# A gated decoder block on one core: x, parameters and weights laid out in the order in which the kernel reads them

## The chip, the cores and the metric

The kernel runs on one core of one Trainium2 chip. The metric is the device time of one execution in microseconds. The profiler records one execution: when each instruction of each engine ran, what ended its waits, and what the core's 16 DMA engines moved. The engines are called as in the profile: PE (TensorE, matmuls), PEld (its weight loads), DVE (VectorE), ACT (ScalarE), POOL (GpSimd) and SP (SyncE, which here only issues DMAs).

## The reference

One decoder block on x of 1 x 256 x 4096 in float32, cut to what matters (b, s, d are batch, sequence and channels; `w_in` is 4096 x 20480, `w_branch` 2 x 2048 x 4096, `w_out` 4096 x 4096):

```python
h = rmsnorm(x, norm_w)                     # over the 4096 channels of a token
proj = h @ w_in
u_p, z_p, u_c, b_c, c_c, z_c, g_logit = split(proj, ...)   # six of 2048, one of 8192
y_pool = causal_multiscale_pool(u_p, pool_w, pool_scale) * silu(z_p)
y_conv = causal_gated_shortconv(u_c, b_c, c_c, conv_w, conv_b) * silu(z_c)
br = einsum('bsnc,ncd->bsnd', stack([y_pool, y_conv], axis=2), w_branch)
gates = sigmoid(g_logit.reshape(b, s, 2, d) + gate_b)
x = x + sum(gates * br, axis=2) @ w_out
return rmsnorm(x, final_norm_w)
```

## The kernel before

Every large product is cut into units of 1024 output columns: 20 units of `w_in`, 8 of `w_branch`, 4 of `w_out`, run one after the other. A unit is a list of steps (class `Step`). A step takes 256 rows of the weights by 1024 columns, which is one megabyte, and multiplies them with the matching 256 channels of the operand for all 256 tokens.

Float32 accuracy comes from splitting each number into a high part (rounded to `F32R` by ACT) and a low part (the rest, by a DVE subtraction), and from three products: high by high, high by low, low by high. A matmul is 128 x 128 by 512 columns. A step of kind **P** does 24 of them. A step of kind **S** does the same 256 x 1024 block with seven products in place of eight (Strassen-like sums of blocks of the operand and of the weights), 21 matmuls, and needs sums of blocks on both sides: `Q3`, `Q5`, `Q6`, `Q7` of the operand, made once for each operand by `sums_s`, and sums of weights, made by DVE for each step. A step of kind **N**, in the first unit only, is a P step whose two halves of k go to different banks (24 matmuls).

The operand x lies in `arena` as `x_ops`: 16 pairs of blocks of 128 channels, 9 in P form, 7 in a form that S steps can use. P form is x times `norm_w`, not yet divided by the root mean square of the token; that factor, `rin`, is applied when the sums are taken out of PSUM (`evacuate`). For the S form the sums that go to the shared banks must hold the factor already (`rbc` and `std`: the factor and its inverse, spread over partitions by PE at L968).

The order of the work is written out when the program is built. `pump` prepares steps up to three ahead of the one that PE runs (`AHEAD`): it issues the load of the step's megabyte on SP's queue into one of three `raw` buffers (`issue_load`; the buffer must have been prepared three steps before), and lets ACT and DVE write the high and low parts into `ring`, a ring of 60 blocks of 256 columns, of which a P step needs 16. Work that is to lie ahead of a step's preparation is hung on it with `before(i, fn)`. Lines L65 (`act`), L68 (`tt`), L80 (`stt`), L83 (`load`) and L87 (`move`, POOL's queue) are helpers, so most operations carry one of these lines, and L1158 is the one line of all matmuls of steps.

In the first unit x itself is still to be turned. x is loaded by tokens (256 rows of 4096), into the homes `R`, `E`, `Y` and again `R`, a quarter each; for each pair p, `turn(p)` (L980) has PE transpose four 128 x 128 blocks into PSUM, and `x_direct` (pairs 0 to 9) writes high and low parts from there. Pairs 10 to 15 are turned by `x_stage`, stored back, and made into S form by `x_sums` and `x_fill`, the N steps of the first unit using them. Pair 9 is made into S form by `x_second` at step 19. `square` makes the sums of squares of the tokens from x by tokens, on ACT and DVE. `norm_w`, `conv_w` and `conv_b` are loaded as rows of 128 and transposed by PE (L933, L937). `make_bands` builds the masks for the pooling on POOL and DVE, at step 21. From the second unit on (`cc0`, whose six S steps are steps 21, 23 and so on to 31) the matmuls are all P and S steps.

Of the kernel before, what the change touches and what calls it, by code (L numbers as in the profile page):

```python
# [56 lines left out]
def hybrid_block(ctx: ExitStack, tc: tile.TileContext, x, norm_w, w_in, pool_w, pool_scale,  # L57
                 conv_w, conv_b, gate_b, w_branch, w_out, final_norm_w, out):
    nc = tc.nc
    xf, of = x[0], out[0]  # L60
    win, wbr, wout, pw = w_in[0], w_branch[0], w_out[0], pool_w[0]
# [51 lines left out]
    ssq = sb("ssq", [P, 2, 8])  # L113
# [20 lines left out]
    def xs(a, b, t=None):  # L134
        q = xhome[a // NU]
        s = slice(a % NU, (b - 1) % NU + 1)
        return q[:, :, s] if t is None else q[:, t, s]

    def load_x(a, b, queue=None):
        pin((queue or nc.sync).dma_start(xs(a, b), xrows[:, :, a:b]))  # L140
# [15 lines left out]
    rows, ones, std = (op.tile([P, P], F32, name=n) for n in ("rows", "ones", "std"))  # L156
    rbc = op.tile([P, T], F32, name="rbc")
    warm = V[:, 0, 0:P].bitcast(BF16)
    rows_n = V[0:32, 1, 0:P]
# [65 lines left out]
    class Step:  # L225
        def __init__(self, unit, kind, src=None, op=None, **kw):
            self.unit, self.kind, self.src, self.op = unit, kind, src, op
            self.__dict__.update(kw)
            self.raw = None
            self.ending = False  # L230
            self.pre = []

        def micros(self):
# [3 lines left out]
            def half(n):  # L237
                def f(block):
# [14 lines left out]
            if self.kind in "PN":  # L253
                self.blocks, self.h, self.l = [None] * 2, [None] * 2, [None] * 2
                return self.pre + [(8, None, half(0)), (8, None, half(1))]
            if self.kind == "S":
# [29 lines left out]
                return self.pre + [(0, None, sums), (12, None, direct), (8, None, t13), (8, None, t24)]  # L286
# [31 lines left out]
        def groups(self):  # L318

            gs = []  # L320
            if self in steps[0:2]:

                for n in range(2):
                    for i in range(3):
                        for k in range(2):
# [5 lines left out]
            elif self.kind in "PN":  # L331
# [3 lines left out]
                for t, n in order:  # L335
                    mm = {"E": [], "F": []}
                    for k in range(2):
                        ah, al = self.op.standing(k, t)
                        h, l = self.h[n][:, k], self.l[n][:, k]
                        mm["F" if self.kind == "N" and k == 0 else "E"] += [(ah, h), (ah, l), (al, h)]  # L340
                    gs += [[(b, t, n), mm[b], None] for b in "FE" if mm[b]]
# [24 lines left out]
    class Unit:  # L366
        def __init__(self, name, src, seq, ops, epi, scaled=False, before=None, dst=None):
# [5 lines left out]
            for kind, i in seq:  # L373
                if kind in "PSN":
                    self.steps.append(Step(self, kind, src(i).rearrange("(k p) n -> p k n", p=P), ops[i],
# [3 lines left out]
                elif kind == "M":  # L379
                    self.steps.append(Step(self, "M", pw[i].rearrange("(k p) n -> p k n", p=P), g=i % 2))  # L380
            self.s = any(st.kind == "S" for st in self.steps)
            self.n = any(st.kind == "N" for st in self.steps)
            main = [st for st in self.steps if st.kind in "PSN"]
# [3 lines left out]
            for st in main:  # L387
                if st.kind in "PN":
                    for t in range(2):
                        for n in range(2):  # L390
                            for k in "FE":
                                b = (k, t, n)
                                more = (6 if k == "E" else 0) if st.kind == "P" else 3
                                self.total[b] = self.total.get(b, 0) + more
# [18 lines left out]
    def evacuate(u, t):  # L413

        dst = E if u.s or u.n else u.dst
# [27 lines left out]
    def combine(u):  # L443
# [9 lines left out]
        elif u.n:  # L453
            for i in range(4):
                cs = slice((i % 2) * NH, (i % 2 + 1) * NH)
                add(d[:, i // 2, cs], shared(i), E[:, i // 2, cs])
# [70 lines left out]
    for o in all_ops:  # L527
        o.standing = standing_p(o)
    for i in range(NP_X, NP_X + NB):
        x_ops[i].standing = standing_s(x_ops[i], ((7, 8), (A12, A22)))  # L530
# [36 lines left out]
    seq_0 = [("P", i) for i in range(NP_X + NB)] + [("N", i) for i in range(NP_X + NB, NP_X + NS_X)]  # L567
# [821 lines left out]
```

## Time and profile before

| | |
|---|---|
| median of 3 runs | 2405.05 us (2404.59 to 2405.11) |
| the profiled execution | 2405.06 us, span 2403.4 us |
| busy PE, DVE, ACT, POOL (share of the span) | 99%, 87%, 56%, 3% |
| DMA | 538.73 MB, mean 224 GB/s |
| granted TensorE clock, mean | 0.999 |

The span goes from the first to the last instruction. A group's line gives engine, operation, out<-in and the count (x), then busy time, the mean ns of one, and the idle time of the engine just before with its releaser. PE's ends are modelled and overlap, so a matmul's mean is longer than the distance between two. The windows view lists, for a stretch, the busy time and the count of each engine, then the granted clock, the DMA engines' busy share and GB/s. The timeline gives start, length, engine, line, operation, tiles and count; in brackets stands the idle time before it and who ended it.

### The profile page before, as it was taken

What the parts mean: (1) busy time and instruction counts of PE and PEld (TensorE: products, weight loads), DVE (VectorE), ACT (ScalarE), POOL (GpSimd) and SP (SyncE); (2) the same over time, 40 slices, a digit from 0 to 9 for tenths busy, and PEclk for the clock granted to TensorE, in tenths of its full rate; (3) what the DMA queues carried; (4) which work ended last, traced back from release to release, by engine and by line L of the source; (5) the groups of instructions that cost most, each with busy time, mean ns of one, the idle gap of its engine ahead of it and who ended that gap; (6) DMA issues with size and microseconds to landing.
All of it is one profiled execution on the core that took longest, in us unless ns stands there. A gap on an engine that the chain in (4) does not pass through costs nothing.

```text
span 2403.4 us, 27936 instructions
## 1 busy us (share of the span) xinstructions
PE 2388.5 (99%) x10666; PEld 1976.7 (82%) x10666; DVE 2095.2 (87%) x2090; ACT 1353.5 (56%) x1406; POOL 62.1 (3%) x137
## 2 busy tenths in 40 slices
PE   9999999999999999999999999999999999999998
PEld 7888888888888888888888888888888888888886
DVE  7899988988989868968999899889888886799998
ACT  6555554555556455555555555555564555555564
POOL 0000000000000000000000000000000001000000
PEclk9999999999999999999999999999999999999999
DMA  7555565655566546556665656566766678656767
GB/s 294 182 201 199 210 234 198 230 196 197 216 234 224 204 177 227 197 198 219 232 237 215 236 204 234 202 249 233 261 235 243 214 255 288 209 203 243 253 214 271
DMA packets 138998, 538.73 MB, mean 224 GB/s; under 512 B 9008, under 2 KB 9584, under 8 KB 135536
## 3 DMA queue, kind: packets, MB, share of 16 engines
q1 hardware_dynamic: 127200, 483.42, 55.1%
q0 software_dynamic: 11328, 52.47, 6.4%
q8 instruction: 83, 1.36, 0.2%
q10 hardware_dynamic: 336, 1.07, 0.1%
q14 instruction: 51, 0.42, 0.1%
HBM read 511.75 MB, written 25.17 MB: 223 GB/s over the span
## 4 chain that ended last, share of the span: by engine, by line
PE 95%; DMA 2%; DVE 2%; ACT 1%; issue 0%; SPq 0%; DVEq 0%; ACTq 0%
PE sums L1158 75%; PE shared L1158 19%; PE shared L685 1%; DMA raw<-in_w_in_dram 1%; DMA raw<-in_w_out_dram 1%; DVE ring L68 1%; PE shared L467 1%; ACT ring L65 0%; DVE R L68 0%; PE shared L980 0%; PE shared L664 0%; DVE V L68 0%; DVE raw L68 0%; PE shared L665 0%; PE shared L667 0%
## 5 line engine op out<-in xcount | busy, mean ns | idle before, releaser
L1158 PE MATMUL sums<-ring,arena 128*128 128x512 f32 x8220 | 1932.1, 390 | 1.8 <-ACT arena L65 0.9
L1158 PEld LDWEIGHTS sums<-ring,arena 128*128 128x128 f32 x8220 | 1539.6, 188 | 322.7 <-ACT ring L65 1.5
L65 ACT ACTIVATE ring<-raw 128x1024 fp32r<-128x1024 f32 (+2 forms) x901 | 989.2, 1136 | 758.6 <-PE sums L1158 277.6
L68 DVE TENSOR_TENSOR ring<-raw,ring 128x1024 fp32r<-128x1024 f32 (+2 forms) x901 | 1162.3, 1322 | 231.0 <-ACT ring L65 199.1
L1158 PE MATMUL shared<-ring,arena 128*128 128x512 f32 x2004 | 507.2, 389 | 0.0
L1158 PEld LDWEIGHTS shared<-ring,arena 128*128 128x128 f32 x2004 | 376.1, 188 | 78.2 <-DVE ring L68 0.2
L65 ACT ACTIVATE ring<-V 128x1024 fp32r<-128x1024 f32 (+1 forms) x167 | 174.1, 1042 | 113.3 <-DVE V L68 77.0
L68 DVE TENSOR_TENSOR V<-raw 128x1024 f32<-128x1024 f32 x164 | 199.7, 1218 | 2.5 <-DMA raw<-in_w_out_dram 2.5
L68 DVE TENSOR_TENSOR ring<-V,ring 128x1024 fp32r<-128x1024 f32 (+1 forms) x167 | 200.7, 1202 | 0.3 <-ACT ring L65 0.2
L68 DVE TENSOR_TENSOR raw<-raw 128x512 f32<-128x512 f32 x164 | 113.5, 692 | 5.7
L68 DVE TENSOR_TENSOR raw<-V,raw 128x512 f32<-128x512 f32 x164 | 113.4, 691 | 5.0
L68 DVE TENSOR_TENSOR R<-R,E 128x1024 f32<-128x1024 f32 (+1 forms) x55 | 95.0, 1744 | 3.2 <-DMA E<-gates_d 2.3
L65 ACT ACTIVATE E<-sums,rin 128x512 f32<-128x512 f32 (+1 forms) x60 | 47.2, 827 | 30.1 <-PE sums L1158 29.7
L68 DVE TENSOR_TENSOR R<-R,shared 128x512 f32<-128x512 f32 x84 | 57.3, 683 | 1.1
L65 ACT ACTIVATE arena<-sa 128x512 fp32r<-128x512 f32 (+3 forms) x32 | 20.3, 644 | 38.9 <-DVE sa L68 33.7
L68 DVE TENSOR_TENSOR R<-R,Y 128x1024 f32<-128x1024 f32 (+1 forms) x28 | 40.3, 1445 | 0.0
L68 DVE TENSOR_TENSOR arena<-sa,arena 128x512 fp32r<-128x512 f32 (+3 forms) x32 | 22.4, 709 | 11.9 <-ACT arena L65 11.9
L65 ACT ACTIVATE R<-R 128x2048 f32<-128x2048 f32 x8 | 15.3, 1914 | 14.5 <-DVE R L68 14.5
L467 PEld LDWEIGHTS shared<-ident,R 128*128 128x128 f32 x160 | 19.4, 140 | 4.2
L467 PE MATMUL shared<-ident,R 128*128 128x128 f32 x160 | 22.6, 272 | 0.0
L685 PE MATMUL shared<-ring 128*128 128x512 f32 x96 | 22.1, 389 | 0.0
L685 PEld LDWEIGHTS shared<-ring 128*128 128x128 f32 x96 | 18.0, 188 | 3.7
(161 smaller groups left out, 431.7 us busy)
## 6 DMA issues: line engine op xcount, KB each, us to landing
raw<-in_w_in_dram SPq DMA_DIRECT2D x319, 1024.0 KB, 4.8
raw<-in_w_branch_dram SPq DMA_DIRECT2D x64, 1024.0 KB, 5.6
raw<-in_w_out_dram SPq DMA_DIRECT2D x64, 1024.0 KB, 5.3
gates_d<-R POOLq DMA_DIRECT2D x8, 1024.0 KB, 5.2
raw<-in_pool_w_dram SPq DMA_DIRECT2D x4, 1024.0 KB, 5.0
Y<-in_gate_b_dram POOLq DMA_DIRECT2D x8, 512.0 KB, 6.2
Y<-gates_d POOLq DMA_DIRECT2D x4, 1024.0 KB, 8.4
E<-gates_d POOLq DMA_DIRECT2D x4, 1024.0 KB, 5.1
```

The source lines that it names most:

```text
L65: return pin(nc.scalar.activation(dst, src, func, **kw))
L68: return pin(nc.vector.tensor_tensor(out=dst, in0=a, in1=b, op=op))
L467: pin(nc.tensor.transpose(shared(j)[:, i * T + t * P:i * T + (t + 1) * P], src[:, t, c:c + P], ident))
L685: pin(nc.tensor.matmul(o, a[:, k, ts], b[:, k], start=(k, i) == (0, 0), stop=(k, i) == (3, 2)))
L1158: pin(nc.tensor.matmul(ps, lhs, rhs, start=n == 0, stop=n == u.total[b] - 1))
```

## The change

The inputs are laid out anew on the host, before the launch: `x_t` holds x by channel (for each partition 16 pairs of 2 x 256 tokens), so that PE transposes no x; `norm_t` and `conv_t` hold the parameters by channel; `w_in`, `w_branch` and `w_out` hold for each step 128 x 2048 numbers in one run (8 KB for each partition, where it was two rows of 4 KB far apart), and `pool_w` likewise. x by rows stays an input for the residual.

In the kernel `turn`, `x_stage`, `x_fill`, the N steps and the second home of part of the operands at the ring's end go. All 16 steps of the first unit are P steps with x in P form from `x_direct`; pairs 10 to 15 keep their first block in slots 0 and 1, which the S sums overwrite later. `x_sums` and `x_parts` make the S form in place, for pairs 10 to 15 with steps 14, 15, 16, 17, 19 and 21 and for pair 9 with step 28. Squares are taken by channel: ACT squares, DVE adds to `sq`, and PE sums over partitions with four matmuls of one column (`sum_squares`), at the start of step 10; the norm's small chain follows it, and the spread comes at the start of step 11. `make_bands` moves from step 21 to step 33. The order of the first loads changes: a quarter megabyte of weights, then the first pair of x, then the rest; x follows pair by pair between the weights (`x_with`), its last quarter on SP's queue at step 6. The convolution's parameters are loaded at step 6, with no transpose.

The diff, cut to its core:

```diff
-    def xs(a, b, t=None):
-        ...
+    def xc(a, b=None):
+        q = flat(xhome[a // 4])[:, a % 4 * 2 * T:((b or a + 1) - 1) % 4 * 2 * T + 2 * T]
+        return q if b else q.rearrange("p (k c) -> p k c", k=2)
     def load_x(a, b, queue=None):
-        pin((queue or nc.sync).dma_start(xs(a, b), xrows[:, :, a:b]))
+        pin((queue or nc.sync).dma_start(xc(a, b), x_t[:, a:b].rearrange("p q k c -> p (q k c)")))
...
                     if self is steps[0] and n == 0:
+                        act(self.h[n][:, 0], q[:, 0])
+                        x_direct(0)
                         for k in range(2):
-                            act(self.h[n][:, k], q[:, k])
-                        for k in range(2):
+                            if k:
+                                act(self.h[n][:, k], q[:, k])
                             sub(self.l[n][:, k], q[:, k], self.h[n][:, k].bitcast(F32))
...
-    seq_0 = [("P", i) for i in range(NP_X + NB)] + [("N", i) for i in range(NP_X + NB, NP_X + NS_X)]
+    seq_0 = [("P", i) for i in range(NP_X + NS_X)]
...
-            return win[2 * i * P:(2 * i + 2) * P, col:col + NU]
+            return win[col // NU, i]
...
-            return wbr[n][2 * i * P:(2 * i + 2) * P, c * NU:(c + 1) * NU]
+            return wbr[n, c, i]
...
-            return wout[2 * i * P:(2 * i + 2) * P, cs]
+            return wout[c, i]
...
-    pin(nc.scalar.dma_start(rows_n, norm_w[0].rearrange("(k p) -> k p", p=P)))
-    move(rows[0:48, :], conv_w[0].rearrange("n (k p) -> (n k) p", p=P))
-    move(rows[48:64, :], conv_b[0].rearrange("(k p) -> k p", p=P))
+    pin(nc.scalar.dma_start(par_n, norm_t))
+    pin(nc.vector.memset(rout, 0.0))
+    act(rout, rout)
...
     def square(c):
-        for t in range(2):
-            ...
+        src = xc(2 * c, 2 * c + 2)
+        if c == 0:
+            act(sq, src, AF.Square)
+        else:
+            act(flat(V), src, AF.Square)
+            add(sq, sq, flat(V))
+        if c == 7:
+            add(sq[:, 0:2 * T], sq[:, 0:2 * T], sq[:, 2 * T:])
+    def sum_squares():
+        for t in range(2):
+            for k in range(2):
+                pin(nc.tensor.matmul(sums_x[:, t:t + 1], sq[:, k * T + t * P:k * T + (t + 1) * P], ones[:, 0:1],
+                                     start=k == 0, stop=k == 1))
...
-    def turn(p):
-        ...
     def x_direct(p):
         o = x_ops[p]
-        b = turn(p)
+        b = xc(p)
...
     def x_sums(p):
-        ...
+        d = direct_at(p)
+        h, l = (x_ops[p].view[:, part].bitcast(F32) for part in range(2))
         add(sa[:, A12:A12 + 2], h[:, A12:A12 + 2], l[:, A12:A12 + 2])
+        add(sa[:, A11:A11 + 2], h[:, d:d + 2], l[:, d:d + 2])
+        both = sa[:, A12:A12 + 4].rearrange("p (k t) c -> p k (t c)", k=2)
+        mul(both, both, rbc[:, None].to_broadcast([P, 2, T]))
         sums_s(sa, [sa[:, i] for i in (A12, A22, A11, A21)])
         mul(sa[:, Q3], sa[:, Q3], std)
+    def x_parts(p):
+        o = x_ops[p]
         for a, b in ((0, 4), (A11, A21)):
             act(o.view[:, 0, a:b], sa[:, a:b])
+        for a, b in ((0, 4), (A11, A21)):
+            sub(o.view[:, 1, a:b], sa[:, a:b], o.view[:, 0, a:b].bitcast(F32))
...
+    squares = {2: 0, 3: 1, 4: 2, 5: 3, 6: 4, 7: 5, 8: 6, 9: 7}
+    seconds = {14: 10, 15: 11, 16: 12, 17: 13, 19: 14, 21: 15, 28: 9}
+    for i in range(1, n0):
+        before(i, x_direct, i)
+    for i, c in squares.items():
+        after(i, square, c)
+    before(6, load_x, 12, 16)
+    before(6, move, par, conv_t)
+    at(10, sum_squares)
+    at(10, rstd)
+    at(10, diagonals)
+    at(10 + 1, spread)
+    at(10 + 1, spread_out)
+    for i, p in seconds.items():
+        before(i, x_sums, p)
+        after(i, x_parts, p)
+    before(33, make_bands, 0)
...
-            for k in range(2):
-                load(q[:, k, 0:NH], s.src[:, k, 0:NH])
+            load(q[:, 0, 0:NH], s.src[:, 0, 0:NH])
+            load_x(0, 1)
+            load(q[:, 1, 0:NH], s.src[:, 1, 0:NH])
             load(q[:, :, NH:NU], s.src[:, :, NH:NU])
...
+    x_with = {0: (1, 2), 1: (2, 4), 3: (4, 6), 4: (6, 8), 5: (8, 10), 6: (10, 12)}
...
+    def by_step(w, pairs, units):
+        return w.reshape(pairs, 2, P, units, NU).transpose(3, 0, 2, 1, 4)
+        ...
+        "x_t": i["x"][0].T.reshape(D // T, 2, P, T).transpose(2, 0, 1, 3),
+        "norm_t": i["norm_w"][0].reshape(-1, P).T,
+        "w_in": by_step(i["w_in"][0], D // T, -1),
```

More of the change, by code (lines that the diff above doesn't have):

```diff
@@ L155, in hybrid_block @@
     op = replace_by("opening")
[L156 removed]
+    diag, ones, std = (op.tile([P, P], F32, name=n) for n in ("diag", "ones", "std"))
     rbc = op.tile([P, T], F32, name="rbc")
     warm = V[:, 0, 0:P].bitcast(BF16)
[L159 removed]
     def p_slot(i):
@@ L323, in groups @@
                 for n in range(2):
-                    for i in range(3):
-                        for k in range(2):
+                    order = ((0, 0), (1, 0), (0, 1), (1, 1), (2, 0), (2, 1)) if self is steps[0] and n == 0 else (
+                        [(i, k) for i in range(3) for k in range(2)])
+                    for i, k in order:
                             for t in range(2):
@@ L1084, in hybrid_block, with after, at @@
-    for p in range(NP_X, NP_X + NB):
-        before(n0 + 3 + 2 * (p - NP_X), x_second, p)
-    before(n0 + 3 + 2 * NB, make_bands, 0)
+    def after(i, fn, *args):
+        steps[i].post.append((0, None, lambda _: fn(*args)))
+    def at(i, fn, *args):
+        steps[i].first.append(lambda: fn(*args))
+    squares = {2: 0, 3: 1, 4: 2, 5: 3, 6: 4, 7: 5, 8: 6, 9: 7}
+    seconds = {14: 10, 15: 11, 16: 12, 17: 13, 19: 14, 21: 15, 28: 9}
+    n0 = len(units[0].steps)
+    for i in range(1, n0):
+        before(i, x_direct, i)
@@ L1223, in run_step @@
             return
+        for f in st.first:
+            f()
         while not st.op.ready:
```

191 lines of the change are left out of this document (55 added, 136 removed).

## The prediction, made before the changed kernel ran

> **What bounds the kernel now.** I read the page first: the busy shares, the chain that ended last and the costliest groups.
>
> ```profile
> span 2403.4 us, 27936 instructions
> PE 2388.5 (99%) x10666; PEld 1976.7 (82%) x10666; DVE 2095.2 (87%) x2090; ACT 1353.5 (56%) x1406; POOL 62.1 (3%) x137
> PE 95%; DMA 2%; DVE 2%; ACT 1%; issue 0%; SPq 0%; DVEq 0%; ACTq 0%
> L1158 PE MATMUL sums<-ring,arena 128*128 128x512 f32 x8220 | 1932.1, 390 | 1.8 <-ACT arena L65 0.9
> L1158 PE MATMUL shared<-ring,arena 128*128 128x512 f32 x2004 | 507.2, 389 | 0.0
> ```
>
> PE is nearly always busy, and the chain runs through it. A mean of 390 ns includes overlap with the next matmul, so I take the pace from the chain itself, then the windows view of L1158 (x counts the matmuls that touch a stretch):
>
> ```profile
> 134.52 6.12 PE sums L1158 x27
> ...
> 0.00:13.60 13.60, 6.81 (x25) 4.71 (x25) 1.00 0.82 292
> 13.62:103.29 89.67, 83.50 (x361) 67.24 (x361) 1.00 0.67 245
> 103.30:186.00 82.70, 82.70 (x366) 68.50 (x365) 1.00 0.53 199
> ```
>
> 27 matmuls in 6.12 us are 226.7 ns each. The first unit has 16 steps of 24. The edges of the second stretch were set 0.2 us behind the starts of the 25th matmul (step 1's first, 13.4) and of the 385th (the second unit's first, 103.1). So steps 1 to 15 take 89.7 us, while 360 matmuls at 226.7 ns are 81.6: 8.1 us of that stretch are something else. The second unit's 16 steps (366 matmuls at 226.7 are 83.0) take 82.7: nothing is lost there. After unit 0 PE runs at its pace, so time can be gained in the opening and hardly anywhere else.
>
> **What the 8.1 us are.** The windows view of L980, the transposes of x, and pieces of the chain:
>
> ```profile
> 0.00:103.30 103.30, 9.07 (x64) 7.59 (x64) 1.00 0.69 252
> ...
> 28.21 0.88 DVE arena L80 x2
> ...
> 35.71 0.87 PE shared L980 x8
> ...
> 42.05 1.31 PE shared L980 x12
> ...
> 48.85 0.87 PE shared L980 x8
> 49.73 0.45 PE shared L968 x4
> ```
>
> There are 64 transposes at 0.87/8 = 0.109 us each. Eight run before step 1, so 56 x 0.109 = 6.1 us lie in the stretch. The spreading of the norm (L968) takes 0.45. The other 1.5 are the parameter transpose (about 0.2) and a wait near 28 us for the low parts of x, because a megabyte of weights landed late behind 3 MB of x.
>
> **Edit 1: no transposes.** All 64 go. In their place PE gets four matmuls of one column for the sums of squares. No such row exists; the nearest is L968's 0.11 each, and I take 0.1 each with a short restart, 0.45 in all (bounds 0.2 and 1.0). The spread stays at 0.45. N steps become P steps with the same 24 matmuls: nothing. Steps 1 to 15 become 81.6 + 0.45 + 0.45 = 82.5: **7.2 us gained**, if nothing else is late.
>
> **Edit 2: the opening's order.** The timeline, the start:
>
> ```profile
> 1.13 2.31 PE L925 MATMUL shared<-V 128*128 128x256 bf16 x10 [1.13 <-DVE V L919]
> 3.74 1.11 PE L980 MATMUL shared<-ident,R 128*128 128x128 f32 x4
> 4.37 0.63 ACT L65 ACTIVATE ring<-raw 128x512 fp32r<-128x512 f32 x1 [0.45 <-DMA raw<-in_w_in_dram]
> 5.79 1.20 PE L1158 MATMUL sums<-ring,arena 128*128 128x512 f32 x2
> 7.12 0.63 ACT L65 ACTIVATE ring<-raw 128x512 fp32r<-128x512 f32 x1 [2.12 <-DMA raw<-in_w_in_dram]
> 7.80 2.57 PE L1158 MATMUL sums<-ring,arena 128*128 128x512 f32 x10 [0.81 <-ACT ring L65]
> 10.57 3.23 PE L1158 MATMUL sums<-ring,arena 128*128 128x512 f32 x13
> 12.06 2.01 ACT L65 ACTIVATE ring<-raw 128x1024 fp32r<-128x1024 f32 x2 [0.31 <-DMA raw<-in_w_in_dram]
> ```
>
> Two matmuls run, then PE waits until the second piece of weights lands at 7.1; 2 + 10 + 13 make 25, the last of them step 1's first. The windows view gives the DMA share and GB/s in its last two columns, and section 3 of the opening's DMA view what was in the way:
>
> ```profile
> 2.00:3.50 1.50, 1.50 (x8) 0.84 (x6) 0.00 (x0) 0.58 (x1) 0.69 (x2) 1.00 0.90 310
> 3.50:5.50 2.00, 1.94 (x9) 1.50 (x10) 0.53 (x2) 0.83 (x2) 0.00 (x0) 1.00 0.72 184
> 8.00:20.00 12.00, 12.00 (x60) 9.99 (x60) 9.24 (x14) 8.71 (x15) 0.00 (x0) 1.00 1.03 413
> rows<-in_conv_w_dram POOLq DMA_DIRECT2D x1, 24.0 KB, 4.7
> ```
>
> The rate falls from 310 to 184 GB/s while POOL's small parameter loads are under way. The change moves these to step 6. Step 1's weights have 1.5 MB ahead of them in the SP queue, as now, 2.6 MB (in 10^6 bytes) with their own: 0.47 by 3.5 us at 310, the rest at 400 by 8.9, landed by about 9.5 to 10; ACT's high half (1.0) then allows step 1 at 10.5 to 11. PE's own side: x's four transposes (1.11) leave the path to the first matmul; x and the first piece land by 4.3, DVE's high part takes 0.44, first matmul near 4.9. The ten warming matmuls take 231 ns for 256 columns, as much as 512 columns take later: PE runs at half its pace here. So some 6 of step 0's 24 cost 0.45 us, until about 7.3, and 18 at 0.227 end near 11.4. I take step 1 at 11.2 in place of 13.4: **2.2 us gained** (bounds: 0, all as now, and 2.9).
> The Trainium skill, "TensorE: Matmul & The Clock Gate", Part 1, says the array runs at half clock until a busy window of about 3.4 us has passed, and that idle time shuts it again; the row agrees on the half pace. By that rule a new wait in step 0 could hold all 24 at half pace, an estimate of 24 x 0.227 = 5.4 us worse.
>
> **Edit 3: vector work moved.** Squares now go on top of steps 2 to 9, conversions of seven x operands to steps 14 to 17, 19, 21 and 28, and make_bands from step 21 to 33. Prices, from the timeline: low parts of x, weights' low halves, one conversion as it is done now for one operand, and the first and last DVE operation of make_bands.
>
> ```profile
> 15.44 0.87 DVE L80 SCALAR_TENSOR_TENSOR arena<-shared,par_n,arena 128x256 fp32r<-128x256 f32 x2
> 30.34 2.35 DVE L68 TENSOR_TENSOR ring<-raw,ring 128x1024 fp32r<-128x1024 f32 x2
> 108.65 0.75 DVE L68 TENSOR_TENSOR sa<-arena 128x256 f32<-128x256 f32 x2
> 109.31 0.75 DVE L68 TENSOR_TENSOR sa<-sa,rbc 128x256 f32<-128x256 f32 x2
> 110.10 1.02 DVE L68 TENSOR_TENSOR sa<-sa 128x128 f32<-128x128 f32 x4
> 111.16 0.29 DVE L68 TENSOR_TENSOR sa<-sa,std 128x128 f32<-128x128 f32 x1
> 112.15 0.89 DVE L68 TENSOR_TENSOR arena<-sa,arena 128x512 fp32r<-128x512 f32 x2 [0.70 <-ACT arena L65]
> ...
> 117.97 0.27 DVE L645 TENSOR_REDUCE cnt<-sa 128x1 f32<-128x128 f32 x1
> ...
> 122.81 0.22 DVE L655 CAST bands<-sa 128x128 fp32r<-128x128 f32 x1
> ```
>
> Steps 3 to 9 cost DVE 2.35 + 0.87 + 1.2 (adding a square of 1024 columns, half of the 2.35 for two such operations) = 4.4 against PE's 24 x 0.227 = 5.44: DVE gains 1.0 a step. Walking it from step 2 (DVE done as PE gets there), it is 7.7 us ahead at step 9 and about 9 at step 13, where the ring of 60 blocks stops it near 11. The norm's chain sits behind step 12's preparation on DVE and ACT; it begins when PE's four small matmuls open step 10 (near 60.1) and is some 3.5 us long (one table load of 1.3, a square root, six small DVE operations), so the spread that opens step 11 (65.9) finds it done, 1.7 to spare; 5 us of PE queue would stand behind it if not. A conversion costs 3.7 to 3.8. Steps 14 and 15 then cost DVE 7.0, 16 and 17 6.2: its lead goes 9.4, 7.4, 5.7, 5.0, 4.2, and is 8.6 again at step 20. From step 21 pairs of S and P steps cost it about 9.2 against PE's 10.2; with the conversions at 21 and 28 the lead stays above 4. make_bands holds DVE 5.1 us (117.97 to 123.0, part of it waiting for POOL's masks), now ahead of a P step in unit 2, where the lead is again about 4 after it; its POOL work moves with it, and nothing else is due on POOL then but a store or two. So this costs nothing as long as 4 us of lead hold; below zero each us is a us of PE. Unit 0's four sums of shared and E (2.5 us of DVE) go.
>
> **Edit 4: each weight load one run.** Section 6, KB and us to landing:
>
> ```profile
> raw<-in_w_in_dram SPq DMA_DIRECT2D x319, 1024.0 KB, 4.8
> raw<-in_w_branch_dram SPq DMA_DIRECT2D x64, 1024.0 KB, 5.6
> raw<-in_w_out_dram SPq DMA_DIRECT2D x64, 1024.0 KB, 5.3
> E<-gates_d POOLq DMA_DIRECT2D x4, 1024.0 KB, 5.1
> ```
>
> E<-gates_d already moves 8 KB in one run per partition, in 5.1 us: no faster and no slower than weights in 4 KB runs. A load is asked for two to three steps, 10 us or more, ahead; a few tenths change nothing. What PE loses after unit 0 bounds the gain: about 9,876 of the L1158 matmuls at 226.7 ns are 2238.9 us, and with the other PE work (some 46) the 2288 us to the last matmul leave about 3.5. I take 0.3 of it (bounds -1 and 3.5). The last megabyte of x goes from POOL's queue to SP's, between the loads of steps 8 and 9; it waits until R is free of x's first quarter, which is read by step 3, while the load ahead of it waits for step 5: the weights queued behind it lose its 2.5 us of transfer, with 5 to spare.
>
> **Sum:** 2405.06 (the profiled execution; 1.7 more than its span, and level with the median of 2405.05) - 7.2 - 2.2 - 0.3 = 2395.4.
>
> **The rivals.** (a) The opening stays data bound: step 1 still at 13.4, total 2397.6. For it: the norm's weights now come in runs of 128 bytes, and small runs were in flight when the rate fell to 184. Against: they are 16 KB, and asked for first. The skill ("DMA: Bandwidth & Descriptors", Specifications) puts full rate at 512 bytes and up; no row here isolates it. (b) DVE loses its lead in steps 14 to 17: if a conversion costs 2 us more than the rows say, the 4.2 turn into about -4, total 2399.4. For: DVE is at 87%, four conversions follow each other. Against: unit 0's spare 1.0 a step. (c) Slower: megabytes in one run are read at a lower rate, since they lie in one place of memory. It decides below the kernel's mean rate, 538.73 MB over 2403 us = 224 GB/s; at 215 the bytes alone take 2506. For: nothing seen but the falls in rate; against: E<-gates_d. (d) Loads that land sooner also take the 3.5 us lost after unit 0: 2392.2. That the change does nothing cannot be: 64 transposes are on a PE that does not wait.
>
> **How the numbers follow.** The forecast has 0.61, (a) 0.14, (b) 0.10, (c) 0.06, (d) 0.09. 2391.5 to 2399.5 holds the first, (a), (d) and half of (b). 0.2% is 4.8 us, about what a measurement can tell: the border is 2400.2. Faster: 0.61 + 0.14 + 0.09 + half of (b) = 0.89; same 0.05; slower 0.06.
>
> **What would show it.** In the changed profile: no transposes of x; the 25th matmul near 11.2 and the 385th near 93.7; no PE wait at steps 10 and 11 or after 14; DVE still ahead at step 17; the drop in GB/s between 3.5 and 5.5 gone; weight loads at 4.6 to 5.3 us. A second unit longer than 83 us would make (b) true, loads over 7 us (c), a 25th matmul after 13 (a).

## The result, and the profile after

The changed kernel takes 2400.79 us (median of 20 executions, 2399.49 to 2402.70) against 2405.08 us before (20 executions): a ratio of 0.9982, 95% interval 0.9975 to 0.9988. That is 4.3 us or 0.18% sooner, where 9.7 us were forecast; it lies outside the range, and within the 0.2% that had been given a chance of 0.05. The profiled execution took 2400.08 us, 1.7 more than its span. Its page, and the windows view of L1122, the line that all matmuls of steps have now:

```profile
span 2398.4 us, 27788 instructions
PE 2380.3 (99%) x10608; PEld 1970.6 (82%) x10608; DVE 2101.8 (88%) x2094; ACT 1351.6 (56%) x1392; POOL 61.2 (3%) x135
L1122 PE MATMUL sums<-ring,arena 128*128 128x512 f32 x8292 | 1942.3, 390 | 5.0 <-ACT arena L68 3.3
raw<-in_w_in_dram SPq DMA_DIRECT2D x319, 1024.0 KB, 4.9
E<-gates_d POOLq DMA_DIRECT2D x4, 1024.0 KB, 5.5
...
0.00:12.30 12.30, 5.95 (x25) 4.49 (x26) 1.00 0.81 300
12.32:95.52 83.20, 82.35 (x361) 67.53 (x361) 1.00 0.68 262
95.53:178.20 82.67, 82.67 (x366) 68.50 (x365) 1.00 0.54 202
```

PE has 58 matmuls fewer, and its idle time ahead of step matmuls grew from 1.8 us to 5.0. Step 1 begins at 12.1 us (13.4 before), the second unit at 95.3 (103.1 before), and that unit takes 82.7 us as it did. So the first unit gained 7.8 us, and the end gained only 5.0. Where the rest went is read from the chain that ended last. Pieces that stand in both chains, first of the kernel before, then of the changed one:

```profile
260.21 8.16 PE sums L1158 x36
...
513.72 21.08 PE sums L1158 x93
...
1744.14 8.16 PE sums L1158 x36
...
1831.67 8.16 PE sums L1158 x36
...
2303.54 11.56 PE sums L1158 x51
```

```profile
3.52 7.45 DMA raw<-in_w_in_dram
...
252.44 8.16 PE sums L1122 x36
...
422.12 6.35 DMA raw<-in_w_in_dram
...
507.74 21.08 PE sums L1122 x93
...
1737.94 8.16 PE sums L1122 x36
...
1801.18 6.38 DMA E<-gates_d
...
1827.79 8.16 PE sums L1122 x36
...
2298.95 11.56 PE sums L1122 x51
```

The lead over the kernel before is 7.77 us at 252 us, 5.98 at 508, 6.20 at 1738, 3.88 at 1828 and 4.59 at 2299. Two losses stand out: 1.8 us between 252 and 508 us, nearly all of it near 430, and 2.3 us between 1738 and 1828 us. The second has two parts, as the starts of the matmuls show: PE waits about 1.1 us longer near 1786 us, and at 1816 us there is a new wait of 1.1 us. I call these the losses at 430, 1786 and 1816. The two loads that the changed chain runs through, a weight load of 6.35 us and a load of E of 6.38 us, are the hints. How PE depends on E stands in the changed kernel's timeline: DVE's sum waits for E, and PE's transposes (L466) wait for a later sum of DVE into R.

```profile
1807.66 2.29 DVE L71 TENSOR_TENSOR R<-R,E 128x2048 f32<-128x2048 f32 x1 [2.45 <-DMA E<-gates_d]
...
1817.60 0.66 PE L466 MATMUL shared<-ident,R 128*128 128x128 f32 x4 [0.93 <-DVE R L71]
```

### The profile page after: what moved, and what is told of

Same layout as the page of the kernel before. It is cut to its first block, busy times and chain, and to the rows that moved or that the text cites. A ratio compares the mean times of both kernels' runs of the same rounds, so it can differ in the third digit from the quotient of the medians.

```text
span 2398.4 us, 27788 instructions
## 1 busy us (share of the span) xinstructions
PE 2380.3 (99%) x10608; PEld 1970.6 (82%) x10608; DVE 2101.8 (88%) x2094; ACT 1351.6 (56%) x1392; POOL 61.2 (3%) x135
## 3 DMA queue, kind: packets, MB, share of 16 engines
q8 instruction: 83, 1.36, 0.2%
## 4 chain that ended last, share of the span: by engine, by line
PE 97%; DVE 1%; DMA 1%; issue 0%; ACT 0%; SPq 0%; DVEq 0%; ACTq 0%
PE sums L1122 77%; PE shared L1122 18%; PE shared L690 1%; PE shared L466 1%; DMA raw<-in_w_in_dram 1%; DVE ring L71 0%; DMA E<-gates_d 0%; DVE R L71 0%; ACT ring L68 0%; PE shared L669 0%; PE shared L670 0%; PE shared L672 0%; SPq L86 0%; DVE raw L71 0%; DVE V L71 0%
## 5 line engine op out<-in xcount | busy, mean ns | idle before, releaser
L1122 PE MATMUL sums<-ring,arena 128*128 128x512 f32 x8292 | 1942.3, 390 | 5.0 <-ACT arena L68 3.3
L1122 PEld LDWEIGHTS sums<-ring,arena 128*128 128x128 f32 x8292 | 1553.6, 188 | 328.3 <-ACT ring L68 2.5
L1122 PE MATMUL shared<-ring,arena 128*128 128x512 f32 x1968 | 497.1, 389 | 0.0
L1122 PEld LDWEIGHTS shared<-ring,arena 128*128 128x128 f32 x1968 | 369.5, 188 | 76.6
L68 ACT ACTIVATE ring<-V 128x1024 fp32r<-128x1024 f32 x164 | 173.2, 1056 | 115.4 <-DVE V L71 76.3
L71 DVE TENSOR_TENSOR ring<-V,ring 128x1024 fp32r<-128x1024 f32 x164 | 199.9, 1219 | 0.3 <-ACT ring L68 0.2
L68 ACT ACTIVATE arena<-sa 128x512 fp32r<-128x512 f32 (+2 forms) x41 | 22.4, 567 | 49.1 <-DVE sa L71 44.0
L71 DVE TENSOR_TENSOR arena<-sa,arena 128x512 fp32r<-128x512 f32 (+2 forms) x41 | 24.5, 616 | 11.9 <-ACT arena L68 11.9
L466 PEld LDWEIGHTS shared<-ident,R 128*128 128x128 f32 x160 | 19.3, 140 | 5.4 <-DVE R L71 1.3
L466 PE MATMUL shared<-ident,R 128*128 128x128 f32 x160 | 22.7, 273 | 0.9 <-DVE R L71 0.9
```

The lines of the kernel that those rows point to most:

```text
L68: return pin(nc.scalar.activation(dst, src, func, **kw))
L71: return pin(nc.vector.tensor_tensor(out=dst, in0=a, in1=b, op=op))
L466: pin(nc.tensor.transpose(shared(j)[:, i * T + t * P:i * T + (t + 1) * P], src[:, t, c:c + P], ident))
L1122: pin(nc.tensor.matmul(ps, lhs, rhs, start=n == 0, stop=n == u.total[b] - 1))
```

## The experiments

Theories after the result: **ring phase** for 430 (the first unit turns over a ring of 60 places, not 54, so later units begin at other places and their preparation is ordered otherwise), **long packets** for 1786 and 1816 (loads in runs of 8 KB are late where other transfers run), **short runs** for the opening (the norm's 128-byte runs). Rival to all: the gain is given back because another engine's chain does not move. Each time stands beside the kernel before in the same group of runs (2405.40, 2405.20, 2404.54 and 2404.99 us in the four groups):

| run | edit to the changed kernel | median us | below before |
|---|---|---|---|
| e1_ring | ring begun at 48 | 2398.35 | 7.05 |
| e2_norm | norm in 512-byte runs | 2401.33 | 4.07 |
| e3_oldw | big weights in the old layout | 2402.22 | 3.18 |
| e4_mb4 | megabyte together, 4 KB runs | 2401.45 | 3.95 |
| e5_after | none | 2400.55 | 4.65 |
| e6_before | (the kernel before) | 2405.27 | -0.07 |
| e7_wonly | (the kernel before, new weight layout) | 2403.03 | 2.17 |
| e8_ringwarm | ring at 48, 13 warm-up products more | 2395.91 | 9.29 |
| e9_ringsplit | ring at 48, warm-up in 13 more pieces | 2396.59 | 7.95 |
| e10_ringwide | as e8, no more instructions | 2397.68 | 6.86 |
| e11_split | warm-up in 13 more pieces | 2398.61 | 5.93 |
| e12_warm | 13 warm-up products more | 2396.82 | 7.72 |
| e13_first2 | as e9, first megabyte by pieces | 2396.12 | 8.87 |
| e14_first4 | as e9, first megabyte in 4 KB rows | 2396.76 | 8.23 |
| e15_base | as e9 | 2397.41 | 7.58 |

**The ring's phase (e1).**

```diff
 rg = Ring(RING)
+rg.head = 48
```

> The changed kernel with one line more: the weight ring's first place is 48 instead of 0, so that unit 1 begins at place 16 as in the kernel before (in the changed kernel it begins at 24, as unit 0 now turns over a ring of 60 places instead of 54). Theory ring phase: the 1.66 us that the changed kernel gives back at 431 us (PE waits 1.72 us for ScalarE's eviction, which stands behind a weight conversion that the order of ring places put ahead of it) does not arise; about 2399.1 us, 1.7 below the changed kernel, and PE's gap at about 429 us is gone. Rival, the vector and scalar chain there is late by itself and the order does not matter: the gap stays, 2400.8 us. A second rival: the new phase moves the stall to another unit, 2400.8 us with the gap elsewhere.

The timeline at 430 us, of the changed kernel and then of e1:

```profile
428.58 1.49 ACT L68 ACTIVATE ring<-raw 128x1536 fp32r<-128x1536 f32 x1 [0.62 <-DMA raw<-in_w_in_dram]
429.97 1.09 ACT L68 ACTIVATE E<-sums,rin 128x1024 f32<-128x1024 f32 x1
431.12 2.26 PE L1122 MATMUL sums<-ring,arena 128*128 128x512 f32 x8 [1.34 <-ACT E L68]
```

```profile
424.88 8.32 PE L1123 MATMUL sums<-ring,arena 128*128 128x512 f32 x36
428.48 1.12 ACT L68 ACTIVATE E<-sums,rin 128x1024 f32<-128x1024 f32 x1 [1.24 <-PE sums L1123]
429.50 1.48 ACT L68 ACTIVATE ring<-raw 128x1536 fp32r<-128x1536 f32 x1
```

In the changed kernel ACT converts weights first, waits 0.62 us for their load to do so, and only then takes the sums out of the banks that PE needs next. In e1 the eviction comes first, as in the kernel before, and PE runs through. Ring phase holds as to the order: the wait is gone. The time fell by 2.4 to 2.8 us against the two groups of the changed kernel, more than the 1.7 forecast for this wait, and not all of it is this wait: e1's profile has none at 1816 us either (1.1 us in the changed kernel), for a reason given below. The rival falls, since what moved was an order, not an engine's speed. That the order is not the whole of the wait is shown by e11 and e12. The profiled execution of e1 was the slowest of its seven; the section on the clock tells why.

**The norm's runs and the weights' layout (e2, e3, e4, e7).**

```diff
-"norm_t": norm.reshape(-1, P).T,
+"norm_t": _np.tile(norm.reshape(-1, P).T, (1, 4)),       # e2
-"w_in": by_step(w_in, ...), ...
+"w_in": w_in, ...                                        # e3, with w_branch and w_out
-    .transpose(3, 0, 2, 1, 4)
+    .transpose(3, 0, 1, 2, 4)                            # e4
```

e7 is the kernel before with `by_step` and the new `pool_w` alone.

> The changed kernel with the norm weights repeated four times along a row, so that their load has runs of 512 bytes instead of 128. Theory short runs: those 128 packets delay the first loads; without them the first weight piece lands about 0.9 us earlier (near 3.9 us instead of 4.75), step 1 begins near 11.2 us instead of 12.10, and the end comes 0.9 us sooner, 2399.9 us. Rival, the norm's load has as many packets and four times the bytes now, and the packets are what counts: landing times, step 1 and the time as they are, 2400.8 us. Rival, the opening's gain is given back later at a stall that other engines set: step 1 near 11.2 us, time 2400.8 us.

> The changed kernel with w_in, w_branch and w_out in their old layout (runs of 4 KB, rows far apart); x, the parameters and pool_w stay new. Theory long packets: loads in 8 KB packets are later where other transfers run beside them, which gave back 1.05 us at 1786 us and 1.16 us at 1815 us; with the old layout both stalls have the length that they have in the kernel before (1.24 us and none), and the time is 2398.6 us, 2.2 below the changed kernel. Rival, the layout of the weights is of no account and the two stalls come of the shifted timing: 2400.8 us, stalls as in the changed kernel. Rival, the new layout is faster at the opening and at 2226 us: 2401.3 us, 0.5 above the changed kernel.

> The changed kernel with each step's megabyte still in one stretch of memory, but in runs of 4 KB instead of 8 KB. Theory long packets: it is the packet's length that makes a contended load late, so this kernel has the times of the old layout, 2398.6 us. Rival, what counts is that the megabyte lies together: as the changed kernel, 2400.8 us. Rival, neither counts: 2400.8 us here and in the old layout.

> The kernel before with one part of the change alone: each step's megabyte of weights in one run of memory (w_in, w_branch, w_out, pool_w), x by its rows with its transposes as before. From the old-layout run (2402.22 us beside 2400.8 us) the layout of the weights is worth about 1 us: 2404.0 us. Rival, the layout of weights was worth something only where no transposes stand between the opening's steps: 2405.1 us. Rival, 8 KB packets make later loads late and the opening gets nothing: 2406 us or more.

Four times the run length changed nothing: step 1 at 12.46 us, time as the changed kernel's. The length of the runs is not what holds the opening. As e2 has as many packets as the changed kernel, only e13 below rules out their number. Long packets fall: with 4 KB runs the wait at 1786 us comes again (2.1 us in e3, 2.4 in e4), that at 1816 in e3 (1.2 us; none in e4), and the old layout is 1.1 to 1.5 us slower, not 2.2 faster. e7 says the same from the other side: the weights' layout alone gains 2.2 us in the kernel before, where about 1 was forecast (ratio 0.9992, 0.9983 to 1.0001, which just includes no change). So the layout is no loss and probably a gain: by the starts of the matmuls about 0.7 us of it lies in the first unit and 0.6 to 0.7 near 2183 and 2227 us, in e3 as in e7. The losses come from elsewhere.

**Is it one execution's accident? (e5, e6)**

> The changed kernel as it is, once more, for a second profile and for its time on the chip of this group of runs. Theory ring phase: PE again waits 1.3 to 1.8 us for ScalarE at about 430 us, as this follows from the order of the instructions; 2400.8 us. The stalls at 1786 us and 1816 us come again within 0.4 us of their lengths (2.00 and 0.93 us) if the program sets them, and differ by more if they are a matter of one execution's transfers.

> The kernel before as it is, for a second profile: no wait of PE at 431 us. If its short stall at 1793 us (1.24 us) and the absence of one at 1822 us belong to the program, they come again; if they belong to one execution, stalls as in the changed kernel (2.0 and 0.9 us) appear here too, and then no gain was given back there.

No: the changed kernel's second profile has waits of 0.8 us at 429 and 0.4 at 432 (1.5 at 429 in the first, by the starts of the matmuls), 1.9 at 1785 and 1.2 at 1816; the second profile of before has 0.7 at 1792 and none at 1822. The losses come again with the program.

**Keeping PE busy in the opening (e8), and what that uncovered (e9 to e12).**

```diff
-WARM, WARM_1, WARM_2 = 10, 6, 0
+WARM, WARM_1, WARM_2 = 10, 19, 0
```

> The changed kernel with the ring begun at place 48, and 19 instead of 6 of the warm-up products (128x256) ahead of the first step, so that PE is busy from 4.3 us to the first weights at about 6 us. Theory clock: in the ring run PE idled 1.9 us there, and eight products after it took 427 ns instead of 227; with PE kept busy none does, step 1 begins at 12.1 us or sooner in the profile, and the median is 2398.0 us, 0.3 below the ring kernel's, with less spread. Rival, the opening is bound by its data so that slow products are hidden: 2398.4 us. Rival, the products stand in the way of the first step: 2399 us.

It came out 2.1 us below its forecast, and not through the opening: step 1 begins at 12.4 us in its profile, where 12.1 or sooner was expected. The wait at 1785 us had shrunk from 1.8 us in e1 to 0.6, and none came at 1816 us (as in e1), 1.8 ms after the one edit that sets it apart from e1. What the edit changes that far away is the count of PE's instructions. The page's section 3 lists queues that carry instructions:

```profile
q8 instruction: 83, 1.36, 0.2%
```

83 packets of 1.36 MB are 16 KB each. PE runs 10608 matmuls and as many weight loads; 21,216 / 83 = 256 instructions a packet. In the traces of before, of the changed kernel and of e1 and e8 a packet comes whenever PE's count is 129 to 209 past a multiple of 256 (from the sixth packet on), whatever the time is. The Trainium skill ("Trainium Architecture — The Big Picture", The software stack) gives an instruction 64 bytes, and 21,216 of them make the row's 1.36 MB; that the streams are brought in at load time, as it says there, does not fit this row. The change took out 58 matmuls with their weight loads, 116 instructions, nearly half a packet, so every packet meets other work. Section 3 and section 6 of the DMA view around the load of E, of the changed kernel (1801 to 1808 us), then e8 (1798 to 1804):

```profile
q8 instruction: 1, 0.02, 0.9%
...
E<-gates_d POOLq DMA_DIRECT2D x1, 1024.0 KB, 6.4
```

```profile
q0 software_dynamic: 144, 1.05, 51.8%
q1 hardware_dynamic: 66, 0.54, 24.9%
issues: line engine op xcount, KB each, median us to landing
raw<-in_w_branch_dram SPq DMA_DIRECT2D x2, 1024.0 KB, 6.5
E<-gates_d POOLq DMA_DIRECT2D x1, 1024.0 KB, 5.0
```

With a packet of instructions under way E takes 6.4 us, without one 5.0. To tell this from the clock, e9 and e11 cut the same warm-up columns into 13 more instructions and leave PE's wait as it is; e10 bridges the wait with no more instructions; e12 is the longer warm-up without the ring edit.

```diff
-for _ in range(n): matmul(shared(3)[:, 0:2 * P], ..., warm)
+for c in {10: [P] * 20, 6: [P] * 6 + [2 * P] * 3}[n]: matmul(shared(3)[:, 0:c], ..., warm[:, 0:c])  # e9, e11
+for c in {10: [1] * 3 + [2] * 7, 6: [2] * 6}[n]: matmul(..., wide[:, 0:c])    # e10: c x 256 columns
```

> The ring kernel (first place 48) with the 16 warm-up products of 256 columns cut into 26 of 128 and 3 of 256: as many columns, so no more work to bridge PE's wait at 4.3 us, but 13 products more, as many as in the ring kernel with the longer warm-up (2395.91 us). Theory instruction fetch: TensorE's instructions arrive in 16 KB packets on the same DMA engines, one for each 256 instructions; the change took 116 instructions out of the first unit, and the packet near 1745 us now runs in the midst of a burst of weight and gate loads, the one near 1804 us beside the load of E. With 26 instructions more (13 products and their weight loads) the packets come at about 1738 us and 1797 us as in the kernel with the longer warm-up, PE's stall at 1785 us shrinks from 1.8 us to 0.6 us, none is left at 1816 us, and the time is 2396.0 us, up to 1.5 more where products after PE's wait run at half rate. Rival, clock: the longer warm-up's whole 2.4 us came of the bridged wait: 2398.4 us, both stalls as in the ring kernel.

> The ring kernel with the longer warm-up in fewer instructions: 13 products of 512 columns and 3 of 256, as many columns as the 29 of 256 that gave 2395.91 us, but 16 instructions as in the ring kernel. Theory instruction fetch: PE's wait at 4.3 us is bridged and no product runs at half rate, but the packets of instructions lie at about 1744 us and 1805 us again and the stall at 1785 us is 1.8 us or more: 2397.5 us. Rival, clock: all of the longer warm-up's gain is the bridged wait: 2395.9 us.

> The changed kernel (ring begun at 0) with the 16 warm-up products cut into 26 of 128 columns and 3 of 256, nothing else. Theory instruction fetch: the wait at 430 us for ScalarE stays (the ring's order), the stall at 1786 us shrinks from 2.1 us to about 0.6 us and the one at 1816 us goes: 2398.2 us. Rival, these stalls come of when the unit starts, not of the instructions: 2400.7 us.

> The changed kernel (ring begun at 0) with 13 warm-up products more and nothing else. Theory instruction fetch and ring phase: the wait at 430 us stays, those at 1786 and 1816 us shrink as in the split kernel, and PE's wait at 4.3 us is bridged: 2397.6 us, 1.7 above the same with the ring begun at 48 (2395.91 us). Rival, the ring's first place matters only together with the wait in the opening: 2395.9 us.

The same view of e10, 1799 to 1807 us:

```profile
q8 instruction: 1, 0.02, 0.7%
...
E<-gates_d POOLq DMA_DIRECT2D x1, 1024.0 KB, 6.1
```

Instruction fetch holds for the wait at 1816. Over all 17 profiles:

| packet after E's issue | profiles | E to landing | PE's wait |
|---|---|---|---|
| 2.5 to 3.6 us | changed (two), e2, e3, e10 | 6.15 to 6.50 us | 0.85 to 1.22 us |
| 4.7 to 4.9 us | e1, e4 | 5.07, 5.34 us | none |
| 0.9 to 1.5 us before it, or none within 8 us | before (two), e7, e8, e9, e11 to e15 | 5.01 to 5.30 us | none |

Cutting the warm-up into more pieces, with no work added, removed the wait (e9, e11), and joining it again with more columns brought it back (e10), at times close to those expected for the theory (2396.59, 2398.61 and 2397.68 us; 2396.0, 2398.2 and 2397.5 expected); e12 came out 0.8 us below its forecast. In e1 and e4 PE ran at half clock for about 3 us near 1790 (next section), so that its packet, which follows PE's count, came a microsecond or more later against E, when most of E had landed; that e1 has no wait at 1816 is luck of this execution, since e10, with the ring and the instruction count of e1, has one. At 1786 the packet is a part only: PE waits 1.4 to 2.4 us in the seven profiles with a packet in the burst of loads at 1743 to 1747 us, and 0.2 to 1.6 in the ten without. Of those ten, the five with the ring begun at 48 have 0.2 to 0.9, and the two with it at 0 (e11, e12) 1.5 each. The 0.6 us expected there of e11 and e12 is a miss. Why the ring's phase tells there is open: the order of ACT's and DVE's instructions is the same by then.

The packets also bear on the wait at 430 us, which was expected to stay in e11 and e12. The matmuls lose only 0.8 us there in these two, against 1.5 to 2.2 in the five profiles that have the ring begun at 0 and the changed kernel's instruction count (the changed kernel's two, e2, e3, e4). The weight loads that ACT waits for differ. Sections 3 and 6 of the DMA view around these loads in the changed kernel (419.8 to 428.6 us), section 6 in e11 (420.6 to 428.2), where section 3 has no q8, and e11's timeline:

```profile
q8 instruction: 1, 0.02, 0.9%
...
raw<-in_w_in_dram SPq DMA_DIRECT2D x3, 1024.0 KB, 6.4
```

```profile
raw<-in_w_in_dram SPq DMA_DIRECT2D x3, 1024.0 KB, 5.1
...
428.20 1.49 ACT L68 ACTIVATE ring<-raw 128x1536 fp32r<-128x1536 f32 x1 [0.17 <-DMA raw<-in_w_in_dram]
429.59 1.10 ACT L68 ACTIVATE E<-sums,rin 128x1024 f32<-128x1024 f32 x1
```

In the five a packet comes at 420.7 to 423.1 us, among the loads; in e11 and e12 it comes at 418.7 and 418.4, before them, and the conversion ahead of the eviction waits 0.17 us or not at all, where it waited 0.62 in the changed kernel. With the ring begun at 48 nothing is lost there, even where a packet lies among the loads (e1, e10). So the order makes the wait possible and costs about 0.8 us by itself; the rest is the packet's.

**The clock.** The windows view (last columns: granted clock, DMA share, GB/s) of e1, then of e8:

```profile
4.30:6.00 1.70, 0.06 (x1) 0.02 (x1) 0.45 (x2) 1.13 (x2) 0.00 (x0) 1.00 0.99 325
8.00:10.50 2.50, 2.50 (x7) 1.92 (x7) 1.41 (x3) 1.85 (x3) 0.00 (x0) 0.50 0.99 416
...
1789.00:1792.10 3.10, 3.10 (x9) 2.42 (x8) 2.10 (x2) 2.54 (x4) 0.00 (x0) 0.50 0.38 148
```

```profile
4.30:6.00 1.70, 1.70 (x10) 1.26 (x9) 0.35 (x2) 1.04 (x2) 0.00 (x0) 1.00 1.00 367
8.00:10.50 2.50, 2.50 (x13) 2.07 (x12) 1.82 (x4) 1.64 (x3) 0.00 (x0) 1.00 0.99 413
```

In e1 PE idled 1.7 us at 4.3 and about 1.8 us at 1785, and each time, some 2 us after the wait had ended, ran at a clock of 0.50 for about 3 us: 13 matmuls of 427 ns instead of 227 (six in the opening, where e8's forecast counted eight), 2.6 us. That explains the slow profiled execution. The changed kernel's two profiles have the same waits and no such stretch; e4, e11, e13 and e14 have 2 to 6 such matmuls, in e11, e13 and e14 from the first product of step 0 on. Where the wait is bridged (e8, e10, e12) no step's matmul runs so, and executions lie within 1.0 to 1.3 us of each other, against 1.8 to 3.2 in the changed kernel, e1, e9, e11 and e15 (5 or 6 executions each against 6 to 20; e13, not bridged, has 1.3 too, and e14 3.4). The Trainium skill ("TensorE: Matmul & The Clock Gate", Part 1) says the window that decides, about 3.4 us, runs freely, so that the same kernel pays differently from run to run; the runs agree, but here waits of 1.7 to 1.8 us were enough. Bridging and pieces together gained 3.1 us without the ring edit (e12 against e5) and 2.2 with it (e8 against e1). Each beside its group's kernel before, pieces alone are 0.9 (e9 against e1), 1.3 (e11 against e5) and 2.4 (e8 against e10); bridging alone is 1.8 (e12 against e11), 1.3 (e8 against e9) and -0.2 (e10 against e1). What bridging is worth in time is therefore not settled.

**The opening (e13, e14, e15).** Step 0's megabyte alone in another layout, on e9:

```diff
+"w_first": w0.reshape(2, P, 2, NH).transpose(2, 0, 1, 3).reshape(4, P, NH),   # e13: four pieces, 2 KB rows
+"w_first": w0.reshape(2, P, NU),                                             # e14: 4 KB rows
```

> The kernel of the split warm-up (ring begun at 48, 2396.59 us) with step 0's megabyte alone laid out piece by piece in the order of its loads, each row of 512 numbers (2 KB) right behind the one before; all later steps as in the change. Theory first pieces: the first loads take 112 GB/s between 2.0 and 3.5 us because their 2 KB rows lie 8 KB apart in the new layout (279 GB/s there with the old layout of w_in); with this layout the first piece lands near 3.7 us instead of 4.8, the first product starts near 5.0 us instead of 6.0, step 1 at 11.5 us or sooner instead of 12.13, and the time is 2396.0 us. Rival, step 1 is bound by its own megabyte (landed at 10.96 us): first product near 5.0 us, step 1 at 12.1, time 2396.6 us. Rival, the slow stretch has nothing to do with the layout of the first megabyte: all as it was.

> As the kernel with step 0's megabyte laid out piece by piece, but in rows of 4 KB one behind the other, of which the first loads take halves. Theory first pieces: rows 4 KB apart are read nearly as fast as rows 2 KB apart (with all weights in such rows the first piece landed at 3.48 us): first piece near 3.5 us, first product near 5.0 us, step 1 at 11.5 us or sooner, 2396.0 us. Rival, step 1 is bound by its own megabyte: 2396.6 us. Rival, distance does not matter: first piece at 4.8 us.

> The kernel of the split warm-up (ring begun at 48) once more, as the base of this group and for a second profile: 2396.6 us; first piece near 4.8 us, step 1 at 12.1 us; the instruction packets near 1737 and 1796 us, the load of E in 5.0 to 5.3 us, and no stall of PE at 1816 us.

The windows view of the changed kernel, of e3 (old layout) and of e13, and e13's chain:

```profile
2.00:3.50 1.50, 1.50 (x9) 1.07 (x8) 0.00 (x0) 0.73 (x2) 0.81 (x17) 1.00 0.57 112
3.50:5.50 2.00, 1.22 (x6) 0.56 (x4) 0.00 (x0) 0.64 (x2) 0.00 (x0) 1.00 1.00 346
```

```profile
2.00:3.50 1.50, 1.50 (x9) 1.07 (x8) 0.00 (x0) 0.74 (x2) 0.81 (x17) 1.00 0.93 279
```

```profile
2.00:3.50 1.50, 1.50 (x17) 1.50 (x15) 0.00 (x0) 0.73 (x2) 0.81 (x17) 1.00 0.88 265
3.50:5.50 2.00, 1.68 (x10) 1.17 (x8) 0.93 (x3) 1.54 (x3) 0.00 (x0) 1.00 0.82 278
...
3.17 7.78 DMA raw<-in_w_in_dram
12.09 49.25 PE sums L1123 x216
```

The slow start, 112 GB/s, does come of the first pieces' 2 KB rows lying 8 KB apart: with them together the rate is 265, with halves of 4 KB rows 317 (e14), beside 147 and 139 in the base (e9, e15), and the first product starts at 5.04 us instead of 6.0. The norm's 128 packets are still there in e13, so they do not make the start slow. But step 1 begins at 12.09 all the same. Its megabyte lands at 3.17 + 7.78 = 10.95 us, as in the changed kernel (3.52 + 7.45 = 10.97), for the rate sags later instead. The rival holds: step 1 is bound by its own data. In e14 that megabyte lands at 11.79 us and step 1 begins at 12.93, where 11.5 or sooner was expected. e13 is 1.3 us below e15 and e14 0.6; e9 and e15, one kernel, differ by 0.4 beside their kernels before and by 0.8 as they stand, and single executions of e15 by 2.1, so that a gain is not shown. e15's second profile agrees with e9's on packets, E and the wait at 1816.

e8, the changed kernel with one line and one constant, has the lowest median: 2395.91 us, ratio 0.9961 to the kernel before (0.9948 to 0.9973). With five or six executions each, e13 (0.2 us more) and e9 (0.7 more) are not told apart from it.

## Why the prediction was wrong, step by step

**The pace** was right: the second unit takes 82.67 us (82.7 forecast), and in the first unit time was gained.

**Edit 1, no transposes, 7.2.** Steps 1 to 15 fell from 89.7 to 83.2 us: 6.5. The mechanism is right; the term for the sums of squares was mis-sized:

```profile
L963 PE MATMUL shared<-ones,sa 128*128 128x1 f32 x8 | 0.9, 240 | 0.0
L972 PE MATMUL shared<-diag,ones 128*128 128x128 f32 x2 | 0.4, 272 | 0.0
```

The four matmuls are eight instructions in the trace and hold PE 0.80 us (61.24 to 62.04), where 0.45 stood with its bound at 1.0. The spread came in time and cost 0.36. The other 0.4 is not told apart.

**Edit 2, the opening, 2.2.** Step 1 at 12.1 instead of 11.2: 1.3 gained. What failed is the sum of bytes, in its rate and in what it counted. The rate was taken as 310 GB/s to 3.5 us and 400 from there; it was 112 and 346 in the two stretches shown above, and then (changed kernel):

```profile
5.50:8.00 2.50, 1.99 (x9) 1.61 (x10) 2.44 (x5) 1.52 (x3) 0.00 (x0) 1.00 1.06 392
8.00:10.97 2.97, 2.97 (x15) 2.35 (x14) 2.02 (x3) 1.47 (x3) 0.00 (x0) 1.00 0.99 412
```

These four stretches move 3.1 MB by the time the megabyte has landed, where the sum has 2.6: loads issued behind it, from 4.08 us on, ran beside it. So a repaired start (e13), which gets 278 GB/s in the second stretch, lands it no sooner. The megabyte landed at 11.0, not 9.5 to 10; the 1.0 from there to step 1 was right (1.1). A second slip: the convolution's load, hung on step 6, has nothing ahead of it on POOL's queue and was issued at 1.5 us, in the opening after all. Rival (a), still data bound, was right in kind; its cause, the norm's runs, is refuted by e2 and e13, and so is what was drawn from the Trainium skill's ("DMA: Bandwidth & Descriptors", Specifications) rule on 512 bytes for this 16 KB load.

**Edit 3, vector work moved, nothing.** The foreseen places held: PE waits for nothing at steps 10, 11 and 14 on, and (b) did not come. But the end of the ring's second home, part of the change, has no term in the sum. It moved the ring's phase and put a conversion ahead of an eviction at 430 us. The wait there cost 1.8 us in the profile; about 0.8 of it stays where no packet of instructions lies among the loads (e11, e12).

**Edit 4, weights in one run, 0.3.** Too small: 1.1 to 1.5 (e3) and 2.2 (e7), inside the bound of 3.5; about 0.7 of it lies in the first unit, for which the term has nothing. (c) is refuted: the loads land in 4.9 us (4.8 before).

**What PE loses after the first unit** was taken as about 3.5 us, of which edit 4 was to save 0.3 (bounds -1 and 3.5); (d) let it only shrink. It grew by 3.2 us. That is the step that failed most: the sum has no term for what shifts behind the first unit when the ring and PE's count of instructions stand elsewhere. From the forecast span, 2393.7, to 2398.4 are 4.7 us. Of these 1.6 lie in the first unit, 3.2 behind it, and 0.3 are what edit 4 was to save, less 0.4 gained after the last matmul. The 3.2 are 1.8 at 430, 1.1 at 1786 and 1.2 at 1816, less 0.2 near 1710, 0.1 near 2183 and 0.6 near 2227 (differences by the starts of matching matmuls). For 430 and 1816 the runs show the cause; at 1786 it is found in part.

With e8's two edits the time is 2395.9, which the forecast of 2395.4 nearly meets. That is luck and no proof of the forecast: e8's parts have gains that it did not hold (the new instruction count, perhaps the bridged wait), and e8 keeps the opening's loss.

## What to carry to other kernels

A change that takes work out at the start shifts everything behind it: before counting the gain at the end, look for what depends on a running count, such as a ring's position that orders an engine's program. PE's instructions come over the same DMA engines as the data, one 16 KB packet for 256 of them, so a transfer on the critical path can become about 1.2 us later because a few dozen instructions far ahead were added or taken away; count them, and try one or two alignments. Dummy products that filled the wait in the opening kept the clock up in all three kernels that had them; the time that this saved was between nothing and 1.8 us.

## What was not expected of the hardware

The instruction packets: E's load takes 6.15 to 6.50 us with one under way 2.5 to 3.6 us after its issue, and 5.0 to 5.3 in other cases of the same load. PE at half pace for about 3 us after waits of only 1.7 to 1.8 us, in some executions and not in others. And the first loads at 112 to 155 GB/s when they begin with 2 KB rows of weights that lie 8 KB apart (the changed kernel and its variants that keep this), 265 to 317 when they lie 2 or 4 KB apart (e13, e14), 279 in the old layout.
